# A depthwise convolution on TensorE, regrouped from spans of 8 tokens by 16 channels to spans of 16 tokens by 8 channels, with its matrices spread on chip; z slabs moved; layer norm sums on VectorE

## The chip, the cores and the metric

The kernel runs on all eight cores of one Trainium2 chip, one sequence of the batch on each core, with no exchange between cores. The metric is the time of the slowest core in device microseconds. A program on all eight cores has a second, slower state in some executions (one die at a lower granted TensorE clock). Such runs are marked slow and are left out here. Different chips were used for different groups of runs; each group has its own runs of the kernel before, and ratios are taken inside a group.

Some runs that count as fast are disturbed in a smaller way: one pair of cores shows a mean clock of 0.97 to 0.98 while the others are above 0.98, and the run is some 14 to 22 us longer. This holds for the run of 1688.55 us of e1_runs, that of 1683.27 us of h1_bigpk, and among the runs of the kernel before for the one of 1691.08 us beside e1_runs and four of the seven beside l1_uact. Where a ratio is called "undisturbed" below, these runs are left out; it is the mean of the rest over the mean of the rest, worked out by hand, without an interval.

Engine names in the profile: PE is TensorE (matmul), PEld its weight loads, DVE is VectorE, ACT is ScalarE, POOL is GpSimd, SP is SyncE, which here only issues DMAs. "PEclk" is the granted TensorE clock, 1.00 being full.

## The reference, cut to what matters

```python
xn   = rmsnorm(concat(meta, x), norm_g)               # 16 + 2048 tokens, 2048 channels
v, g, z_c, u, z_s, gl_c, gl_s = split(xn @ w_in)      # 5 x 1024 and 2 x 2048 columns
# branch A: Conformer convolution
a = v * sigmoid(g)
a = causal_depthwise_conv(a, dw_w) + dw_b             # width 31, 1024 channels
a = layernorm(a, ln_g, ln_b)                          # over the 1024 channels
y_c = silu(a) * silu(z_c)
# branch B: S5 state space block (64 groups of 16 channels), gelu, GLU, silu(z_s)
y_s = ...
merged = sigmoid(gl_c + b) * (y_c @ w_conv) + sigmoid(gl_s + b) * (y_s @ w_ssm)
out = rmsnorm(h + merged @ w_out, final_g)[:, 16:]
```

## The kernel before

Everything runs in one pass per core. In time order: x is loaded and normalised while the first projections run (0 to 150 us); then the state space stage (150 to 550 us), in which TensorE alternates between projections (`u`, `vg`, then `z`), the convolution and the state space blocks, and VectorE and ScalarE work for the blocks; then the rest of the `z` slabs, the layer norm and the GLU (to 784 us); then the gates, the two branch projections and the output projection, all 512 columns wide, to the end.

A small list scheduler in the kernel's own source places every instruction on its engine from estimated durations and priorities; the engines then execute these fixed orders.

The convolution is done as banded matrices. The input goes to a scratch tensor in HBM (`a_scr`) and comes back with 8 tokens by 16 channels on the 128 partitions; five 128x128 matrices per group of 16 channels do the 31 taps. The matrices are prepared on the host, mostly zeros, and loaded:

```python
for gp in range(4):                                   # of block m, eight blocks in all
    tz, tzB = TZ[tz_n[0] % 3]
    dma("pool", [(tz, w_dw[4 * m + gp])], ...)        # 320 KB in bf16, twice that in HBM
    z4 = tz.rearrange("p (g d c) -> p g d c", g=2, d=5)
    for gg in range(2):
        g = 2 * gp + gg
        mms([(ps[bk][:, gg * 256:gg * 256 + 256], z4[:, gg, d, :], a3[:, g, 4 - d:260 - d], d == 0, d == 4)
             for d in range(5)], 256, (tzB, a2B), (psB[bk],), prio=14)
    ...                                               # ScalarE moves PSUM out, with scale and bias
```

The layer norm sums over channels, which lie on partitions, are products with a matrix of ones on TensorE, 64 matmuls of 512 columns:

```python
for n in range(4):
    act(sq3, CBv[:, :, n * 512:(n + 1) * 512], AF.Square, n=4096, ...)
    mms([(ps[b1_], ones_b[:, :], CBv[:, m, n * 512:(n + 1) * 512], m == 0, m == 7) for m in range(8)], 512, ...)
    mms([(ps[b2_], ones_b[:, :], sq3[:, m, :], m == 0, m == 7) for m in range(8)], 512, ...)
```

The projections' results leave PSUM through ScalarE or VectorE into small buffers (11 of them, shared), and from there SP issues their stores to scratch:

```python
bk = main_bank()                                      # one of three PSUM banks
proj(wv, wB, 0, lambda k: XMv[:, k, lo:lo + NC], NC, xb_of(lo, lo + NC), bk)
pi, pt, pB = chunk_piece()
cp("act", pt[:, 2:NC + 2], ps[bk][:, 0:NC], n=NC, reads=(psB[bk],), writes=(pB,), prio=1)
dma("sp", [(u_scr[m][j], pt[:, 2:NC + 2])], f"pc{pi}", 128 * NC * 2, (pB,), (uscB[m][j],), prio=5, store=True)
```

## Time and profile before

| | before |
|---|---|
| time, fast runs | 1673.06, 1673.22, 1674.25 us |
| PE busy | 1631 of 1678.5 us |
| state space stage, 150 to 550 us: PE busy, clock | 380 us, 0.97 |
| from 550 us to the gates (784 us) | PE always busy, clock 1.00 |

The first lines are from the page of the kernel before: busy microseconds with the share of the span, then the busy tenths and the granted clock in 40 slices of the span.

```profile
PE 1631.0 (97%) x9426; PEld 928.3 (55%) x9512; DVE 706.7 (42%) x1262; ACT 554.6 (33%) x954; POOL 106.9 (6%) x206
...
PE   7999989998999999999999999999999999999997
...
PEclk9999999999999999999999999999999999999999
```

The table of stretches of the same kernel gives busy time (and number of instructions) of each engine, then clock, DMA share and GB/s.

```profile
core 6: us, PE busy (x) PEld busy (x) DVE busy (x) ACT busy (x) POOL busy (x), PEclk, DMA share, GB/s
...
150.00:550.00 400.00, 379.68 (x3143) 301.20 (x3141) 279.56 (x545) 194.49 (x396) 33.02 (x62) 0.97 0.83 139
550.00:729.20 179.20, 179.03 (x831) 81.34 (x833) 42.73 (x67) 103.98 (x111) 5.81 (x11) 1.00 0.54 133
```

TensorE bounds the kernel; outside the start, what it loses it loses in the state space stage. What it waits for is in the table of waits (total us, times, longest):

```profile
PE ps L446 <- DMA WS<-w_dw: 8.9, 4, 4.2
...
PE ps L446 <- DMA CY<-u_scr: 5.7, 1, 5.7
PE ps L446 <- DVE CY L420: 2.8, 5, 1.0
...
PE ps L446 <- ACT ST L436: 1.0, 1, 1.0
```

And these are groups of instructions, forms kept apart: the convolution's matmuls and the ScalarE copies (busy us, mean ns of one, idle before). The last is the eviction of a `u` tile.

```profile
L446 PE MATMUL ps<-ST,WS 128*128 128x256 bf16 x320 | 41.9, 281 | 10.5 <-DMA WS<-w_dw 8.9 <-DVE ST L437 1.4 <-DVE CY L420 0.2
...
L413 ACT ACTIVATE CY<-SM 128x257 f32<-128x257 f32 x64 | 29.4, 498 | 0.1
...
L413 ACT ACTIVATE CY<-CY,SM 128x514 f32<-128x514 f32 x32 | 22.9, 716 | 0.5
...
L436 ACT CAST ST<-ps 128x258 bf16<-128x258 f32 x64 | 23.7, 372 | 62.5 <-PE ps L446 56.7 <-DMA u_scr<-ST 5.3
```

A mean of a matmul is a latency, not a spacing. The spacing is read from the order in time: ten convolution matmuls of 256 columns start 1.09 us before the next group, 109 ns each.

### The profile page before, as it was taken

To read this page: it belongs to the slowest core of one execution; us is meant where nothing else is said; L and a number is where in the kernel's file an instruction comes from. 1 tells how busy PE (TensorE), PEld (TensorE's weight loads), DVE (VectorE), ACT (ScalarE), POOL (GpSimd) and SP (SyncE) were. 2 spreads that over 40 slices of the span, in tenths; PEclk is the share of its full clock that TensorE was granted. 3 is DMA by queue.
4 is the path that set the end of the run, shared out by engine and by line. 5 is a ranking of instruction groups with operands and counts; after the bars stand their busy time and mean duration, and the time that the engine had idled before them with its cause. 6 is when DMAs were issued, how large, how long until landed. Compare 5 with 4: busy or idle time off the path is not lost.

```text
span 1678.5 us, 25748 instructions; the slowest of 8 cores (1665.3 to 1678.5 us)
## 1 busy us (share of the span) xinstructions
PE 1631.0 (97%) x9426; PEld 928.3 (55%) x9512; DVE 706.7 (42%) x1262; ACT 554.6 (33%) x954; POOL 106.9 (6%) x206
## 2 busy tenths in 40 slices
PE   7999989998999999999999999999999999999997
PEld 6888868887855444444444444444444444444443
DVE  3799158786777110578111111111111221225433
ACT  4564346454455169554111111111111111122222
POOL 1000000010001000000100000000110100100000
PEclk9999999999999999999999999999999999999999
DMA  9935979889577654443644444445555553837612
GB/s 239 218 90 103 144 95 148 143 142 145 110 153 161 160 148 98 113 108 94 113 76 75 76 76 76 76 76 89 100 93 92 101 93 81 184 98 237 215 76 76
DMA packets 115163, 200.86 MB, mean 120 GB/s; under 512 B 19424, under 2 KB 68832, under 8 KB 112864
## 3 DMA queue, kind: packets, MB, share of 16 engines
q0 software_dynamic: 33792, 92.29, 35.2%
q1 hardware_dynamic: 80672, 105.35, 22.9%
q8 instruction: 78, 1.28, 0.3%
q10 hardware_dynamic: 576, 1.58, 0.3%
q14 instruction: 45, 0.37, 0.1%
HBM read 248.92 MB, written 42.53 MB: 174 GB/s over the span
## 4 chain that ended last, share of the span: by engine, by line
PE 89%; DMA 4%; DVE 2%; SPq 2%; issue 2%; ACT 1%; DVEq 0%; ACTq 0%; POOLq 0%
PE ps L446 88%; DMA WS<-w_dw 2%; SPq L458 2%; DVE CY L420 1%; DMA WS<-w_main 1%; DMA CY<-x_t 1%; DMA CY<-u_scr 1%; ACT CY L413 0%; DVE CY L431 0%; PE ps L737 0%; ACT L413 0%; DVE XM L431 0%; DVE ST L431 0%; PE ps L725 0%; DVE CY L979 0%
## 5 line engine op out<-in xcount | busy, mean ns | idle before, releaser
L446 PE MATMUL ps<-XM,WS 128*128 128x258 bf16 (+1 forms) x6144 | 1044.0, 329 | 5.9 <-DVE XM L431 2.2
L446 PEld LDWEIGHTS ps<-XM,WS 128*128 128x128 bf16 x6144 | 603.1, 98 | 409.5 <-issue 12.9
L413 ACT ACTIVATE ST<-ps,SM 128x512 f32<-128x512 f32 (+2 forms) x224 | 137.2, 626 | 622.8 <-PE ps L446 619.2
L431 DVE SCALAR_TENSOR_TENSOR ST<-ps,ST 128x512 f32<-128x512 f32 x132 | 91.3, 692 | 529.1 <-PE ps L446 529.1
L446 PE MATMUL ps<-CY,WS 128*128 128x512 bf16 x1217 | 282.3, 379 | 3.3
L446 PEld LDWEIGHTS ps<-CY,WS 128*128 128x128 bf16 x1280 | 125.1, 98 | 151.1
L420 DVE TENSOR_TENSOR CY<-CY 128x512 bf16<-128x512 f32 (+4 forms) x184 | 120.9, 658 | 28.0 <-PE ps L446 11.4
L413 ACT ACTIVATE ST<-ps 128x258 f32<-128x258 f32 (+1 forms) x136 | 65.0, 483 | 148.7 <-PE ps L446 145.2
L420 DVE TENSOR_TENSOR CY<-ps,CY 128x514 f32<-128x514 f32 (+2 forms) x97 | 66.1, 683 | 109.7 <-PE ps L446 108.8
L413 ACT ACTIVATE CY<-CY 128x514 f32<-128x514 f32 (+3 forms) x112 | 82.3, 751 | 55.9 <-DVE CY L420 30.4
L458 POOL DMA_DIRECT2D WS<-w_main x104 | 55.2, 531 | 684.9 <-PE ps L446 530.2
L420 DVE TENSOR_TENSOR ST<-ST 128x512 f32<-128x512 f32 (+3 forms) x87 | 56.0, 650 | 68.0 <-ACT ST L1090 47.2
L420 DVE TENSOR_TENSOR CY<-CY,ST 128x512 f32<-128x512 f32 (+3 forms) x115 | 64.3, 594 | 14.0 <-DMA CY<-par_b 7.0
L436 ACT CAST ST<-ps 128x258 bf16<-128x258 f32 (+1 forms) x96 | 41.9, 438 | 64.3 <-PE ps L446 58.5
L446 PE MATMUL ps<-CY 128*128 128x256 bf16 (+1 forms) x320 | 52.6, 279 | 8.6 <-DMA CY<-u_scr 5.7
L431 DVE SCALAR_TENSOR_TENSOR XM<-CY,SM,ST 128x258 bf16<-128x258 f32 x128 | 52.8, 483 | 19.2 <-ACT ST L413 19.2
L446 PE MATMUL ps<-XM 128*128 128x512 bf16 (+1 forms) x267 | 56.3, 367 | 0.3
L446 PE MATMUL ps<-CY,XM 128*128 128x512 bf16 x251 | 56.1, 379 | 0.3
L446 PE MATMUL ps<-CY,ST 128*128 128x512 bf16 x251 | 55.2, 380 | 0.3
L446 PE MATMUL ps<-XM,ST 128*128 128x512 bf16 x251 | 55.2, 380 | 0.3
L413 ACT ACT_TABLE_LOAD x35 | 44.9, 1283 | 27.0 <-PE ps L446 13.5
L446 PE MATMUL ps<-ST,WS 128*128 128x256 bf16 x320 | 41.9, 281 | 10.5 <-DMA WS<-w_dw 8.9
(82 smaller groups left out, 799.4 us busy)
## 6 DMA issues: line engine op xcount, KB each, us to landing
WS<-w_main POOLq DMA_DIRECT2D x104, 512.0 KB, 6.3
WS<-w_br POOLq DMA_DIRECT2D x32, 512.0 KB, 6.2
CY<-x_t SPq DMA_DIRECT2D x30, 516.0 KB, 17.6
WS<-w_dw POOLq DMA_DIRECT2D x32, 320.0 KB, 9.5
z_scr<-ST SPq DMA_DIRECT2D x64, 128.0 KB, 3.1
ST<-z_scr SPq DMA_DIRECT2D x32, 256.0 KB, 3.4
WS<-x SPq DMA_DIRECT2D x8, 1024.0 KB, 8.5
CY<-x SPq DMA_DIRECT2D x8, 1024.0 KB, 12.4
```

What stands on the lines that cost most here:

```text
L413: f = lambda e: e.activation(out=out_, in_=in_, func=func, bias=bias, scale=scale)
L420: return S.op(eng, lambda e: e.tensor_tensor(out=out_, in0=in0, in1=in1, op=op), d, reads, writes, **kw)
L431: return S.op("dve", lambda e: e.scalar_tensor_tensor(out=out_, in0=in0, scalar=scalar, in1=in1, op0=op0, op1=op1), 0.15 + n / 960.0, read ...
L436: return S.op("act", lambda e: e.copy(out=out_, in_=in_), 0.22 + n / 1200.0, reads, writes, **kw)
L446: return lambda e: e.matmul(a[0], a[1], a[2], start=a[3], stop=a[4])
L458: return lambda e: e.dma_start(out=o, in_=i, allow_slow_non_contiguous=True)
```

## The change

The intent: with 16 tokens by 8 channels on the partitions, 31 taps need three matrices instead of five, and the moving operand is 128 columns instead of 256. Only the taps are loaded from HBM; ScalarE spreads them into the band matrices by eight copies per half block, each scaled by a column of a 0/1 mask. Four `z` slabs move in among the state space blocks to fill holes of TensorE. The layer norm sums become running sums on VectorE, and TensorE sums only the 128 partitions at the end. The core of the diff:

```diff
-    w_dw = din("w_dw", [32, 128, 1280])
+    w_dw = din("w_dw", [16, 128, 384])
...
-        NPC_, PCB = 11, (NC + 2) * 2
+        NPA, NPU, PCB = 5, 6, (NC + 2) * 2          # store buffers: 5 for a_scr, 6 for u and z
...
-            dma("sp", [(a_scr[m][j], pt)], f"pc{pi}", 128 * PCB, (pB,), (ascB[m][j],), prio=5, store=True)
+            dma("sp", [(a_scr[m][:, j].rearrange("e p c -> p e c"), p3)], f"pa{pi}", 128 * PCB, (pB,), (ascB[m][j],), prio=5,
+                packets=256, store=True)
...
-            for gp in range(4):
-                tz, tzB = TZ[tz_n[0] % 3]
-                dma("pool", [(tz, w_dw[4 * m + gp])], ...)
+            for hf in range(2):
+                tp, tpB = TAP[tz_n[0] % len(TAP)]
+                tz, tzB = TZ[tz_n[0] % 2]
+                dma("pool", [(tp, w_dw[2 * m + hf])], ...)
+                z3 = tz.rearrange("p (x h) -> p x h", h=8)
+                for h in range(8):
+                    act(z3[:, :, h], tp, AF.Copy, scale=mask8[:, h:h + 1], n=384, reads=(tpB, mask8B), parts=(tzB,), prio=15)
+                z4 = tz.rearrange("p (g d c) -> p g d c", g=8, d=3)
+                ...
+                    mms([(ps[bk][:, g * 128:g * 128 + 128], z4[:, 4 * (gq % 2) + g, d, :], a3[:, 4 * gq + g, 2 - d:130 - d], d == 0,
+                          d == 2) for g in range(4) for d in range(3)], 128, (tzB, a2B), (psB[bk],), prio=14)
...
-            if m > 3:
-                vg(m)
+            if 3 <= m < 7:
+                vg(m + 1)
+            for _ in range((1, 1, 1, 1, 0, 0, 0, 0)[m]):
+                z(next(zc))
...
+        for m in range(8):                            # layer norm sums
+            act(s_, c_, AF.Square, bias=dwb(m), n=2048, ...)
+            ...
+                stt(ms, c_, dwb(m), ms, ALU.add, ALU.add, n=2048, ...)
+                tt(vs, vs, s_, ALU.add, n=2048, ...)
```

`z3[:, :, h]`: in bf16 this writes one 2-byte element every 16 bytes. The cut leaves out four smaller parts of the change: the ring of weight slots for the projections shrinks from six to five, the loads of y_scr go to ScalarE's queue, gelu no longer waits for the layer norm, and the scheduler's estimates for short matmuls and transposes are halved.

## The prediction

> **What bounds it now.** TensorE. The page's busy table gives PE 1631 of 1678.5 us (97%); the chain of waits is 88% matmuls. From 550 us on the stretches table shows PE always busy at clock 1.00: 16 matmuls of 512 columns take 3.45 us, 215.8 ns each. The losses lie before: about 29 us at the start (loads, untouched) and the state-space stage, 150 to 550 us, where PE is busy 380 of 400 us at a mean clock of 0.97. Instruction counts times spacings (110 ns for 258 columns, 215.8 for 512) over 150 to 729 us give about 547 of 579 us, so some 32 us are lost to idle and to the low clock behind it. The PE waits name w_dw 8.9 us (longest 4.2), u_scr 5.7 us, VectorE about 4. Other cores lose less (spans from 1665).
>
> **PE work removed.**
> - Convolution: 320 matmuls of 256 columns, 109 ns each = 35 us. After: 384 of 128 columns. Eight 128-column transposes, each with its own weights, span 0.61 us with a latency of 0.22, so 56 ns each: 21.5 us. Saves 13.4.
> - Layer norm sums: 64 matmuls of 512 columns become 16: 48 x 215.8 ns = 10.4 us.
> - Four z slabs as 256-column tiles: under 1 us worse.
> Sum: about 23 us, all on the critical path.
>
> **Stalls.** Conv weights from HBM fall from 32 x 320 KB to 16 x 192 KB, which should remove most w_dw waits and their throttled windows. z slabs fill PE in blocks 0 to 3, where PE stood 5.7 us for u_scr; vg one block earlier takes away waits for a_scr. I expect 15 to 20 of the 32 us back.
>
> **Added, off the path.**
> - ScalarE: 128 spreads of 384 columns. From its 257-column (498 ns) and 514-column (716 ns) copies, about 0.6 us each, 77 us; they write every 16 bytes, and the Trainium skill ("SBUF — State Buffer", the note on 16-byte cachelines) says each new line pays a penalty, so 0.6 to 1.0 us. No instruction of before writes so. ScalarE is busy 194 of 400 us in the stage and would rise to 270 to 320: room, but the convolution now waits for load, then eight spreads, from one tap buffer.
> - VectorE: layer norm sums, 8 x 2.35 + 7 x 2.2 us plus splits, about 43 us, in 550 to 729 us where it is busy 43 of 179; hidden beneath z slabs (166 us for twelve) and the GLU.
> - DMA: a_scr and c_scr rows become 258 and 256 bytes; the skill ("DMA: Bandwidth & Descriptors", Specifications) wants 512. Twice the packets, but less w_dw; only six u/z buffers against 11.9 us landing of a u store could stall PE a few us.
>
> VectorE's work per state-space block is about 38 us, near the block period of 40, so the stage itself ends hardly earlier; the gain appears as more z done inside it, and the gates begin (784 us before) about 40 us earlier. The rest, 890 us, is unchanged.
>
> **Prediction.** 1673 - 23 - 16 = 1634 us, range 1617 to 1652. Faster by over 2%: 0.61; within 2%: 0.36; slower: 0.03.
>
> **Would show it right.** PE busy time down 23 us or more; conv matmuls spaced 56 ns; no w_dw wait on PE; clock 0.98 or better in 150 to 550 us; GLU end near 745 us.
>
> **Would make it wrong.** Conv matmuls spaced near 100 ns (weight loads); PE waiting for spreads on ScalarE, or for u/z buffers behind stores; small-packet DMA delaying u_scr and y loads; layer norm or gelu not finished when z runs out, which would show as PE idle before the GLU or gates.

## The result, and the profile after

Ratios here are the mean time of one kernel's fast runs over that of the other's fast runs of the same rounds, so not quite the ratio of the medians quoted beside them.

| | before | after |
|---|---|---|
| median | 1673.74 us (four runs, one of them slow) | 1784.57 us (1781.28 to 1792.73) |
| ratio, 95% interval | | 1.0669 (1.0632 to 1.0707) |
| PE busy in 150 to 550 us, clock | 380 us, 0.97 | 314 us, 0.89 |
| first matmul of the gates | 784 us | 887 us |

The change made the kernel 6.7% slower. The page of the kernel after:

```profile
PE 1642.4 (92%) x9784; PEld 952.7 (53%) x9784; DVE 749.4 (42%) x1296; ACT 755.0 (42%) x1055; POOL 98.4 (5%) x191
...
PE   7898688877768879999989999999999999999997
...
PEclk9999889989889999999999999999999999999999
```

ScalarE has 200 us more work than before. The slices show where PE has holes now: the third to the fifteenth, which is the state space stage. PE busy went up although it has less to do, because some of it ran at half clock (the granted clock in 220 to 225 us is 0.50; with the spread mended, below, the same 9784 matmuls take 1608.3 us). The stretches:

```profile
150.00:550.00 400.00, 313.63 (x2753) 263.01 (x2751) 220.81 (x440) 312.14 (x397) 15.40 (x29) 0.89 0.46 88
550.00:840.00 290.00, 265.63 (x1597) 153.60 (x1595) 138.57 (x203) 185.35 (x212) 15.87 (x30) 0.98 0.56 120
```

The waits of PE after, where w_dw was first before (L438 is the eviction of `u` tiles, L415 with ST the other evictions, L415 with WS the spread):

```profile
PE ps L448 <- ACT ST L438: 37.4, 15, 6.5
PE ps L448 <- ACT ST L415: 35.2, 14, 7.7
PE ps L448 <- ACT WS L415: 16.2, 4, 8.7
PE ps L448 <- DVE CY L422: 11.8, 6, 9.7
...
PE ps L448 <- DMA WS<-w_br: 7.4, 1, 7.4
```

Two lines of PE's order in time show such waits and the half clock behind them (start, us, what, idle before it). The 24 convolution matmuls take 2.72 us here and 1.51 us at 261.53 us:

```profile
205.95 2.72 PE L448 MATMUL ps<-ST,WS 128*128 128x128 bf16 x24 [8.65 <-ACT WS L415]
...
222.52 3.57 PE L448 MATMUL ps<-XM,WS 128*128 128x256 bf16 x16 [1.13 <-ACT ST L438]
```

And the two groups that explain them, the spread and the eviction of a `u` tile:

```profile
L415 ACT ACTIVATE WS<-CY,SM 128x384 bf16<-128x384 bf16 x128 | 239.9, 2102 | 27.0 <-DMA CY<-w_dw 27.0
...
L438 ACT CAST ST<-ps 128x258 bf16<-128x258 f32 x64 | 30.6, 487 | 16.7 <-PE ps L448 16.5
```

A spread takes 2.10 us, where 0.6 to 1.0 us had been forecast and 0.54 us stands in the kernel's own schedule. PE waits for ScalarE 89 us in these three lines (37.4 + 35.2 + 16.2), and most of that is not for the spreads but for evictions; that these were late because they stood behind spreads is what the experiments test. The eviction itself took 487 ns instead of 372 (369 again in e1_runs); why is not shown.

### The profile page after: what moved, and what is told of

Same layout as the page of the kernel before. It is cut to its first block, busy times and chain, and to the rows that moved or that the text cites. A ratio compares the mean times of both kernels' runs of the same rounds, so it can differ in the third digit from the quotient of the medians.

```text
span 1790.9 us, 26522 instructions; the slowest of 8 cores (1767.2 to 1790.9 us)
## 1 busy us (share of the span) xinstructions
PE 1642.4 (92%) x9784; PEld 952.7 (53%) x9784; DVE 749.4 (42%) x1296; ACT 755.0 (42%) x1055; POOL 98.4 (5%) x191
## 4 chain that ended last, share of the span: by engine, by line
PE 75%; ACT 9%; DMA 6%; issue 4%; DVE 4%; SPq 1%; DVEq 0%; ACTq 0%; POOLq 0%
PE ps L448 75%; ACT WS L415 6%; DVE CY L422 2%; DMA a_scr<-ST 2%; ACT CY L415 1%; DMA CY<-w_dw 1%; DMA ST<-a_scr 1%; DMA WS<-w_main 1%; DVE XM L433 1%; SPq L460 1%; DMA CY<-x_t 1%; ACT ST L438 1%; ACT ST L415 1%; DMA WS<-w_br 0%; DVE CY L1015 0%
## 5 line engine op out<-in xcount | busy, mean ns | idle before, releaser
L448 PE MATMUL ps<-XM,WS 128*128 128x258 bf16 (+2 forms) x6400 | 1062.5, 324 | 59.6 <-ACT ST L415 32.4
L448 PEld LDWEIGHTS ps<-XM,WS 128*128 128x128 bf16 x6400 | 632.9, 99 | 453.6 <-issue 68.4
L415 ACT ACTIVATE ST<-ps,SM 128x512 f32<-128x512 f32 (+1 forms) x160 | 109.6, 687 | 580.6 <-PE ps L448 571.6
L415 ACT ACTIVATE WS<-CY,SM 128x384 bf16<-128x384 bf16 x128 | 239.9, 2102 | 27.0 <-DMA CY<-w_dw 27.0
L448 PEld LDWEIGHTS ps<-CY,WS 128*128 128x128 bf16 x1280 | 125.6, 98 | 160.0 <-issue 10.3
L415 ACT ACTIVATE ST<-ps 128x512 bf16<-128x512 f32 (+2 forms) x184 | 93.1, 513 | 138.7 <-PE ps L448 131.1
L415 ACT ACTIVATE CY<-CY 128x514 f32<-128x514 f32 (+3 forms) x112 | 89.5, 816 | 45.5 <-DVE CY L422 29.6
L422 DVE TENSOR_TENSOR ST<-ST 128x512 bf16<-128x512 f32 (+4 forms) x102 | 77.3, 765 | 69.0 <-ACT ST L415 62.7
L448 PE MATMUL ps<-ST,WS 128*128 128x128 bf16 x384 | 32.8, 259 | 33.1 <-ACT WS L415 16.2
L433 DVE SCALAR_TENSOR_TENSOR ST<-ST,ps 128x258 bf16<-128x258 f32 x64 | 26.8, 420 | 81.8 <-PE ps L448 42.7
L438 ACT CAST ST<-ps 128x258 bf16<-128x258 f32 (+1 forms) x96 | 48.5, 517 | 18.4 <-PE ps L448 18.3
L417 ACT ACTIVATE ST<-WS 128x512 bf16<-128x512 f32 x32 | 20.1, 629 | 84.7 <-DVE WS L422 84.1
```

The costliest lines, as they stand in the source:

```text
L415: f = lambda e: e.activation(out=out_, in_=in_, func=func, bias=bias, scale=scale)
L417: f = lambda e: e.activation(out=out_, in_=in_, func=func, bias=bias, scale=scale, accum_out=accum)
L422: return S.op(eng, lambda e: e.tensor_tensor(out=out_, in0=in0, in1=in1, op=op), d, reads, writes, **kw)
L433: return S.op("dve", lambda e: e.scalar_tensor_tensor(out=out_, in0=in0, scalar=scalar, in1=in1, op0=op0, op1=op1), 0.15 + n / 960.0, read ...
L438: return S.op("act", lambda e: e.copy(out=out_, in_=in_), 0.22 + n / 1200.0, reads, writes, **kw)
L448: return lambda e: e.matmul(a[0], a[1], a[2], start=a[3], stop=a[4])
```

## The experiments

Theory A, at first: the 16-byte stride makes the copy slow; evictions queue behind it; that is all of the 110 us. Rivals: B, small packets and few store buffers; C, the copy is slow for its pointer scale or its bf16 source; and later, an order planned for short spreads (e3_model), ScalarE's load even when mended (F), the store queue.

### The spread with runs of 16 elements (e1_runs)

```diff
-                z3 = tz.rearrange("p (x h) -> p x h", h=8)
+                z3 = tz.rearrange("p (y h t) -> p y h t", h=8, t=16)
                 for h in range(8):
-                    act(z3[:, :, h], tp, AF.Copy, ...)
+                    act(z3[:, :, h, :], tp.rearrange("p (y t) -> p y t", t=16), AF.Copy, ...)
...
-            dma("sp", [(c_scr[m].rearrange("e j (h g) r -> (e j h) (g r)", g=16), c2_)], "c2", ...)
+            dma("sp", [(c_scr[m].rearrange("e j (h g) r -> h (e j) (g r)", g=16), c2_)], "c2", ...)
```

> The changed kernel with only the place of the spread weights changed: each of the eight ScalarE copies of a half writes runs of 16 adjacent elements (32 bytes) instead of one element every 16 bytes, the outputs come out in the order channel, token, and the store to c_scr puts them right. Same number of instructions, same order, right result. Theory A (the stride of the writes made a spread 2.10 us instead of about 0.6, and PSUM evictions queued behind it on ScalarE): the spread falls to 0.6 to 0.8 us, ScalarE busy time falls by 150 us or more, PE waits for ScalarE (88 us now) fall below 20 us, and the time falls by over 100 us to 1625 to 1670. Rival B (small-packet stores, six store buffers for u and z): the spread gets short but the time stays above 1730. Rival C (the copy is slow for the pointer scale or for the bf16 source, not for the stride): the spread stays near 2 us and the time near 1784.

Measured: 1665.64, 1667.24 and 1688.55 us (one more run was slow); before on this chip 1668.70 to 1673.57 us, with one of 1691.08; ratio 0.9987 (0.9878 to 1.0095); result correct. From its groups, page and waits of PE:

```profile
L415 ACT ACTIVATE WS<-CY,SM 128x384 bf16<-128x384 bf16 x128 | 72.1, 608 | 29.0 <-DMA CY<-w_dw 29.0
...
PE 1608.3 (97%) x9784; PEld 937.2 (56%) x9784; DVE 747.1 (45%) x1296; ACT 598.3 (36%) x1055; POOL 98.4 (6%) x191
...
PE ps L448 <- ACT ST L438: 8.2, 3, 3.8
...
PE ps L448 <- ACT ST L415: 3.4, 3, 1.5
```

The spread falls from 2102 to 608 ns with the number and order of the instructions unchanged (only the pattern of the c_scr store changes with it), and over 100 us of the loss go with it. PE's waits for ScalarE in the three lines above fall from 89 to 13 us. Theory A stands; B and C as the main cause fall. PE now has 23 us less work than before (1631.0 to 1608.3), as forecast, and yet the undisturbed runs are only 5 us better than those of the kernel before on this chip (1666.4 against 1671.6 us, 0.997). That second gap is taken up below.

### What one copy costs by its access pattern (e5_bench)

Thirteen dummy instructions, four times over, were put into the gates stage of the kernel before, where ScalarE and VectorE have time. Each form has its own element count, so that it can be told in the profile.

> The kernel before, with copies of about 190 elements added in its gates stage, where ScalarE and VectorE have time, to read what one costs: written to adjacent elements, every 2nd, 4th, 8th, 16th bf16 element, every 16 bytes in float32, in runs of 16, read every 16 bytes, with and without the pointer scale; on VectorE adjacent and every 16 bytes; and the whole spread as one product with a mask on VectorE and on GpSimd. Theory A: adjacent 0.44 us; every 8th element near 1.1 us with either scale, runs of 16 near 0.45. Rival C: every form with a pointer scale slow alike. For strides of 4 and 8 bytes I expect something between.

Measured (busy us, then mean ns of one). On ScalarE: 190 elements written side by side; 189 every 2nd element; 188 every 4th; 187 every 8th, which is the change's pattern; 186 the same with an immediate scale; 185 float32 every 16 bytes; 192 in runs of 16; 90 every 16th; 184 read every 8th and written side by side. On VectorE: 182 side by side, 183 every 8th. Last, half a spread as one product with the mask, on GpSimd and on VectorE.

```profile
L413 ACT ACTIVATE ST<-ST,SM 128x190 bf16<-128x190 bf16 x4 | 1.8, 451 | 9.3 <-POOL ST L420 9.3
L413 ACT ACTIVATE ST<-ST,SM 128x189 bf16<-128x189 bf16 x4 | 2.0, 511 | 0.4
L413 ACT ACTIVATE ST<-ST,SM 128x188 bf16<-128x188 bf16 x4 | 2.9, 714 | 0.4
L413 ACT ACTIVATE ST<-ST,SM 128x187 bf16<-128x187 bf16 x4 | 4.5, 1126 | 0.3
L413 ACT ACTIVATE ST<-ST 128x186 bf16<-128x186 bf16 x4 | 4.1, 1030 | 0.3
L413 ACT ACTIVATE ST<-ST,SM 128x185 f32<-128x185 bf16 x4 | 2.5, 625 | 0.4
L413 ACT ACTIVATE ST<-ST,SM 128x192 bf16<-128x192 bf16 x4 | 1.8, 455 | 0.4
L413 ACT ACTIVATE ST<-ST,SM 128x90 bf16<-128x90 bf16 x4 | 2.7, 679 | 0.4
L413 ACT ACTIVATE ST<-ST,SM 128x184 bf16<-128x184 bf16 x4 | 2.5, 618 | 0.3
...
L425 DVE TENSOR_SCALAR ST<-ST,SM 128x182 bf16<-128x182 bf16 x4 | 1.1, 277 | 0.4
L425 DVE TENSOR_SCALAR ST<-ST,SM 128x183 bf16<-128x183 bf16 x4 | 2.5, 636 | 17.0 <-ACT ST L413 17.0
...
L420 POOL TENSOR_TENSOR ST<-ST,SM 128x1536 bf16<-128x1536 bf16 x4 | 11.2, 2806 | 19.1 <-DVE ST L420 19.1
L420 DVE TENSOR_TENSOR ST<-ST,SM 128x1536 bf16<-128x1536 bf16 x4 | 7.0, 1758 | 0.4
```

The stride of the write is the cause: from every 2nd element on, the cost climbs with the distance, to 2.5 times at 16 bytes (1126 against 451 ns). The pointer scale is worth 96 ns of that (1126 against 1030). Runs of 16 cost nothing. A strided read costs far less than a strided write (618 ns). The distance in bytes is not all: float32 at the same 16 bytes took 625 ns, and at 32 bytes a bf16 element costs no more than at 16 (about 4.2 and 4.4 ns each, if some 0.3 us are fixed, as 451 ns for 190 and 608 for 384 adjacent elements say). The mechanism behind this is not shown.

### The suspected cost alone, added to the kernel before (e4_strided, e4_contig, k5_slots)

```diff
-            s = slot_n[0] % 6                        # weight slots; room for the dummy buffer
+            s = slot_n[0] % 5
...
+                for h in range(5):                   # in each of the 32 convolution steps
+                    act(dz3[:, :, :, h], ones..., AF.Copy, scale=mask8[:, h:h + 1], n=256, ...)   # e4_strided: every 16 bytes
+                    act(dzc[:, h], ones..., AF.Copy, scale=mask8[:, h:h + 1], n=256, ...)         # e4_contig: side by side
```

> The kernel before, with 160 ScalarE copies of 256 bf16 elements added among its convolutions, each writing one element every 16 bytes to a buffer that nobody reads (the weight ring is five slots instead of six to make room). Nothing waits for them but what is behind them on ScalarE. Theory A: about 1.4 us each, ScalarE busy up by about 220 us, and the time up by 40 to 110 us, though no convolution waits for a spread: the evictions behind them are enough. A rival, that it hurts only because the convolution waits for its own spreads: the time stays within 15 us of the kernel before.

> Control of the run with strided copies: the same 160 copies of 256 elements, in the same order, written to adjacent elements. Theory A: 0.5 us each, ScalarE busy up by about 75 us, and the time within 15 us of the kernel before. If five slots or the mere number of ScalarE instructions hurt, this run is slow as well.

> Control for e4_contig (1689 to 1696 us): the kernel before with five weight slots instead of six and no copies. If the 71 us of contiguous copies made e4_contig slow, this is at 1668 to 1677; if the lost slot did it, at about 1690.

The two groups of copies, first of e4_strided (with two of PE's waits there), then of e4_contig:

```profile
L413 ACT ACTIVATE WS<-ones_b,SM 128x256 bf16<-128x256 bf16 x160 | 202.6, 1581 | 15.6 <-DMA WS<-w_dw 15.6
...
PE ps L446 <- ACT ST L436: 32.0, 17, 4.8
...
PE ps L446 <- DMA WS<-w_dw: 2.0, 1, 2.0
```

```profile
L413 ACT ACTIVATE WS<-ones_b,SM 128x256 bf16<-128x256 bf16 x160 | 70.8, 503 | 22.3 <-DMA WS<-w_dw 22.3
```

The strided copies, whose results nobody waits for, make the kernel before slow: 1760.36 us, ratio 1.0497 (1.0417 to 1.0576). The contiguous ones in the same order give 1692.15 us, 1.0093 (1.0014 to 1.0172), 68 us less. (The copies also hold the buffers of w_dw until they have run, but PE waits only 2.0 us for w_dw in e4_strided.) PE waits 44.7 us for evictions there (L436 and L413 with ST) and 13.7 us for other results of ScalarE. So what stands behind the copies on ScalarE, evictions above all, is enough; the wait of the convolution for its own matrices is not needed for the loss. e4_contig is slower than I expected (16 to 21 us instead of under 15), and k5_slots accounts for about half of that: five weight slots alone, without any copies, give 1.0058 (1.0024 to 1.0093), on another chip, and PE is busy 418.4 us of 150 to 600 there against 429.6 before. The change also runs with five slots.

### Was it the order? (e3_model)

The changed kernel with the estimate of a spread raised from 0.54 to 1.89 us, so that the order is planned for slow spreads:

```diff
-                    act(z3[:, :, h], tp, AF.Copy, scale=mask8[:, h:h + 1], n=384, ...)    # n only sets the estimate
+                    act(z3[:, :, h], tp, AF.Copy, scale=mask8[:, h:h + 1], n=2000, ...)
```

> The changed kernel as it is, with its 16-byte stride, but the program that lays out the order of instructions is told that a spread takes 1.9 us instead of 0.54. Rival to theory A (not the 240 us of spreads as such, but an order planned for short ones makes PE wait): the time falls by over 40 us. Theory A: ScalarE keeps 755 us of work, of which over 300 fall into 400 us of the state space stage; the time stays above 1750.

Measured: 1743.40 us, ratio 1.0435 (1.0411 to 1.0460). Both readings are partly right: about 40 us are recovered (1.0669 less 1.0435 is 39 us), which is the mark that I had set for the rival, while the 1750 us that I had set as the least for A were missed; 73 us of loss (1743 less 1670) remain. The state space stage is now well fed (PE busy 443 us of 150 to 600, against 351 in the kernel after), but with less of VectorE's work done (busy 240.5 us of 150 to 600, against 290.4 in e1_runs), and the time comes back later: PE waits for the layer norm.

```profile
PE ps L448 <- DVE ST L422: 41.2, 3, 39.3
PE ps L448 <- ACT ST L415: 27.1, 5, 23.9
```

A better plan moves ScalarE's extra work; it can't remove it.

### Spreading on GpSimd (h4_pool)

On e1_runs, the eight copies are replaced by one product with the mask on GpSimd.

```diff
-                for h in range(8):
-                    act(z3[:, :, h, :], ...)
+                tt(z3, tp.rearrange("p (y t) -> p y t", t=16).unsqueeze(2).broadcast_to(sh),
+                   mask8.unsqueeze(1).unsqueeze(3).broadcast_to(sh), ALU.mult, n=2400, ..., eng="pool")
```

> e1_runs with each half's eight ScalarE copies replaced by one product with the mask on GpSimd, from the bench (2.8 us for 1536 elements) about 5.6 us each, 90 us in all on an engine that is idle for 94% of the time; right result. ScalarE busy falls by 77 us. If ScalarE still holds PE up in e1_runs (13 us of waits), the time falls by 5 to 12 us. If GpSimd and VectorE get in each other's way, VectorE's mean times rise and the time does not fall.

Measured: 1725.36 us, ratio 1.0323 (1.0299 to 1.0346), correct. GpSimd takes 5.5 us a half as expected, and VectorE pays. First two of its groups before, then the same two in h4_pool:

```profile
L420 DVE TENSOR_TENSOR CY<-CY 128x257 f32<-128x257 f32 x64 | 27.4, 428 | 5.7
...
L420 DVE TENSOR_TENSOR CY<-ps,CY 128x514 f32<-128x514 f32 x64 | 43.9, 687 | 61.7 <-PE ps L446 61.7
```

```profile
L422 DVE TENSOR_TENSOR CY<-CY 128x257 f32<-128x257 f32 x64 | 58.1, 907 | 5.7
...
L422 DVE TENSOR_TENSOR CY<-ps,CY 128x514 f32<-128x514 f32 x64 | 43.8, 686 | 65.9 <-PE ps L448 65.9
```

An addition of two SBUF tensors takes 907 instead of 428 ns; one with an operand in PSUM is untouched. This agrees with the Trainium skill, "SBUF — State Buffer", section "Who interferes with whom": VectorE and GpSimd take turns, for whole instructions, on a shared pair of SBUF ports, and a VectorE instruction with two SBUF inputs needs the read port of that pair. The trace shows the turns too: around a GpSimd product of 5.43 us (at 161.79 us) two VectorE operations of 512 columns last 6.53 us, and two of the same form take 1.27 us where GpSimd is idle (at 256.28 us).

### Where the rest of the forecast went: one part of the change at a time

With the write mended the time is at 1667 us, not at 1634. These runs undo or change one thing each; all have the order worked out anew, so a few us between two of them can be the order alone.

```diff
# g3_noz, from e1_runs: no z slabs among the blocks
-            for _ in range((1, 1, 1, 1, 0, 0, 0, 0)[m]):
+            for _ in range((0, 0, 0, 0, 0, 0, 0, 0)[m]):
# g4_lnpe, from e1_runs: layer norm sums on TensorE again, as the 64 matmuls shown above (bias left out of the sums)
# h2_lnonly, from the kernel before: only the layer norm sums on VectorE, gelu not held behind the layer norm
# h1_bigpk, from e1_runs: the store's two runs of 260 bytes as one of 520 (wrong place on purpose)
-            dma("sp", [(a_scr[m][:, j].rearrange("e p c -> p e c"), p3)], f"pa{pi}", ...)
+            dma("sp", [(a_scr[m].rearrange("e j p c -> (e j p c)").rearrange("(j p c) -> j p c", j=8, p=128)[j], pt)], f"pa{pi}", ...)
# g1_buffers, from e1_runs
-        NPA, NPU, PCB = 5, 6, (NC + 2) * 2
+        NPA, NPU, PCB = 5, 8, (NC + 2) * 2
# g5_both, from g1_buffers: gate weights no longer held back
-            return wload(s_, src_ap, 33, after=(zm,) if 6 <= g_slot[0] <= 8 else ())
+            return wload(s_, src_ap, 33)
# k1_two, from h1_bigpk: two of the eight copies, the rest stays zero (wrong on purpose)
-                for h in range(8):
+                for h in range(2):
```

> e1_runs without z slabs among the state space blocks (all sixteen afterwards, as before the change). If the slabs fill holes of PE, the time rises by 5 to 20 us and PE stands idle near 200 us, where it stood for u_scr in the kernel before. If they only take buffers and the store queue from u, the time falls by 3 to 10 us.

> e1_runs with the sums of the layer norm as 64 matmuls on TensorE, as before the change (the convolution bias is left out of the sums, so the result is slightly wrong on purpose). By the count of matmuls PE has 10.4 us more; PE is never idle there, so the time should rise by 10 us, less the 7 us wait for w_br if that goes with VectorE's load: 3 to 11 us above e1_runs.

> One part of the change alone in the kernel before: the layer norm sums on VectorE (and gelu no longer held behind them); convolution, z slabs and their order as before. In g4_lnpe against e1_runs this part was worth about 16 us. If it stands alone, PE busy falls by 10 us and the time falls to 1657 to 1664; then the convolution and the z slabs, with the spread mended, gave nothing (e1_runs has 1667). If the gain of e1_runs over the changed kernel is all of conv, this run is at 1668 or above.

> e1_runs with each store of the gated convolution input as 128 runs of 520 bytes instead of 256 runs of 260 (the place in a_scr is then wrong on purpose, and so is the result; the same bytes are read and computed). Theory E (small packets keep the loads of x longer: in 30 to 150 us PE is busy 114 us of 120 in e1_runs against 118 before, and the DMA share in 100 to 120 us is 0.41 against 0.08): PE busy in 30 to 150 us returns to 117 or more, the a_scr waits (4.6 us) shrink, and the time falls by 4 to 10 us. Rival: the early loss comes from the order of the instructions: no change.

> On top of e1_runs (spreads in runs of 16, 1665.6 and 1667.2 us, one run 1688.6): eight instead of six buffers for the stores of u and z, nothing else by hand; the order of the instructions is worked out anew and differs in places. Theory D (of the 39 us that I forecast, 23 came as PE work, but the stalls did not shrink because u and z wait for six buffers behind stores to HBM): the wait of ScalarE for u_scr stores (11.3 us) and of PE for those evictions (8.2 us, then half clock) nearly vanish, and the time falls by 8 to 15 us to about 1655. Rival: the stores are late because the SP queue is jammed, not because buffers are few: waits move to other tiles and the time stays within 4 us of e1_runs.

> g1_buffers with one more edit: the loads of weights for the first gates no longer wait for the last multiplication of the state space output on VectorE. In e1_runs PE waits 6.9 us for w_br there, because VectorE had 152 us of work in 550 to 785 us (89 in the kernel before) and comes to that multiplication later. Theory: this wait is gone and the time is 6 to 10 us below g1_buffers. Rival: the load was late for the traffic of the DMA, not for that wait: no change.

> h1_bigpk (mended spreads, large packets; 1661 to 1663 us) with two instead of eight copies per half; the rest of the band matrices stays zero from one fill, so the result is wrong on purpose. ScalarE falls by about 58 us, nothing else changes. Theory F (with the stride mended the conv part still gives back its 13 us of PE work because its 77 us on ScalarE delay evictions and tables in a stage where ScalarE is on every chain): 8 to 16 us faster, about 1650. Rival: ScalarE has room at 0.6 us a copy, and the loss lies in the order, the six buffers or the store queue: within 4 us of h1_bigpk.

| run | fast runs, us | ratio (95%) | PE busy, us | PE busy in 30 to 150 / 150 to 600 us |
|---|---|---|---|---|
| before | 1673.06 to 1674.25 | 1 | 1631.0 | 117.9 / 429.6 |
| e1_runs | 1665.64, 1667.24, 1688.55 | 0.9987 (0.9878 to 1.0095) | 1608.3 | 114.5 / 428.5 |
| g3_noz | 1667.19 to 1669.46 | 0.9976 (0.9950 to 1.0002) | 1605.9 | 111.5 / 418.9 |
| g4_lnpe | 1681.11 to 1686.41 | 1.0072 (1.0052 to 1.0092) | 1624.5 | 113.0 / 424.7 |
| h2_lnonly | 1656.88 to 1662.67 | 0.9928 (0.9902 to 0.9953) | 1618.5 | 116.5 / 432.3 |
| h1_bigpk | 1661.31, 1661.69, 1663.44, 1683.27 | 0.9979 (0.9911 to 1.0048) | 1607.8 | 116.6 / 429.1 |
| g1_buffers | 1664.37 to 1672.90 | 0.9978 (0.9951 to 1.0004) | 1613.7 | 111.5 / 426.3 |
| g5_both | 1665.74 to 1673.04 | 0.9981 (0.9954 to 1.0008) | 1612.2 | 112.9 / 428.7 |
| k1_two | 1666.59, 1668.49 (others slow) | none | 1608.8 | 115.9 / 427.6 |

What follows:

- The layer norm sums are the part that pays. Alone in the kernel before they give 0.9928, and taking them out of e1_runs costs about 16 us (3 to 11 had been expected). In h2_lnonly the sums come together with the earlier gelu.
- The z slabs among the blocks gain nothing that can be seen (g3_noz against e1_runs). With them the last VectorE scan of the state space blocks ends at 574 us, without them at 528 us: the slabs are done earlier and the blocks later.
- The convolution, mended, gives back its 13 us. e1_runs is not faster than h2_lnonly, which has the old convolution and 10 us more PE work.
- Part of that may be the small packets. With runs of 520 bytes PE is busy 116.6 us of 30 to 150 instead of 114.5, and the DMA share in 100 to 120 us is 0.09 instead of 0.41: the loads of x are through earlier. In the undisturbed runs this is worth about 3 us (0.995 against 0.997), under the 4 to 10 expected; over all runs the two intervals overlap.
- Another part may be the lost weight slot, which I did not test in the changed kernel. In the kernel before it costs 0.6% (k5_slots), some 10 us, about as much as the convolution gives back; b2_taps, below, which also runs with five slots, has 30 us of idle PE in 150 to 600 us where h2_lnonly has 18.
- ScalarE's load is not the main cause once mended. k1_two leaves away 45 us of ScalarE's busy time, and PE is busy 427.6 us of 150 to 600, no more than in h1_bigpk (429.1). My theory F (8 to 16 us) fell by this stretch. The time leaves room for a smaller share: the mean of its two fast runs is 0.992 of the kernel before on its chip, against 0.995 in the undisturbed runs of h1_bigpk, some 5 us, with no interval and on different chips.
- More buffers move the waits (e1_runs' 8.2 us of PE for `u` evictions become 4.5, but the wait for a_scr grows from 4.6 to 6.7 and one of 4.4 for u_scr appears) and gain nothing. Freeing the gate weights (g5_both) does not move the time either, but it is no test of the wait of 6.9 us for w_br in e1_runs: that wait is gone in g1_buffers already, before the gate weights are freed.

In every one of these versions PE stands idle about 18 to 31 us of 150 to 600 us, as before the change (20 us).

### The store queue (l1_uact, l2_uact), and two versions that did not help (b1_onez, b2_taps)

All scratch stores and loads are issued by SP, in order (after the change, all but the loads of y_scr). In the chain of waits of the kernel before, SP's issues hold 34% of 150 to 220 us. The edit issues the `u` stores from ScalarE's queue, in h2_lnonly and in g5_both:

```diff
-                dma("sp", [(u_scr[m][j], ...)], f"pc{pi}", ...)
+                dma("act", [(u_scr[m][j], ...)], f"pu{pi}", ...)
```

> h2_lnonly with the u stores issued from ScalarE's queue instead of SP's, where they stand behind the issues of other stores and loads. If the jammed SP queue makes the wait for u_scr (6.5 us in h2_lnonly, with half clock behind it), it shrinks below 3 us and the time falls by 4 to 8 us against h2_lnonly's ratio of 0.993, to about 0.989. If ScalarE's issue time costs more than it saves, the ratio is 0.993 or above.

> g5_both (mended spreads, eight u and z buffers, gate weights not held back; ratio 0.998) with the same edit. If the store queue is what keeps PE idle for 20 of 450 us in the state space stage of every version so far (k1_two showed that ScalarE's load is not), PE busy there rises by 6 us or more and the ratio falls to about 0.992. If not, the cause of these 20 us stays open.

Measured: l1_uact 1655.62 to 1658.39 us, correct; before on that chip 1676.24 to 1693.90; ratio 0.983 (0.9774 to 0.9885), by the record's rule unclear. Four of those runs of before are disturbed; undisturbed, the ratio is 0.987, where h2_lnonly on its chip has 0.994 worked out in the same way. l2_uact 1656.76 and 1666.13 us, two more runs slow, so no interval (undisturbed about 0.990). PE busy in 150 to 600 us:

```profile
150.00:600.00 450.00, 437.23 (x3460) 329.31 (x3458) 312.27 (x568) 222.38 (x425) 35.23 (x66) 0.99 0.80 147
```

is l1_uact (432.3 in h2_lnonly), and

```profile
150.00:600.00 450.00, 434.23 (x3852) 351.60 (x3850) 295.55 (x577) 275.65 (x536) 26.97 (x51) 0.98 0.67 125
```

is l2_uact (428.7 in g5_both), just under the 6 us that I had set as the mark. So some 5 us of PE's idle time per version go away when SP no longer issues the `u` stores; it is the only thing tried that shrinks it with either convolution (e3_model's 7 us of idle time there are paid for later). Each figure is of one profile and of an order worked out anew, so I take the 5 us as likely and not as shown: l2_uact loses 2.7 us in 30 to 150 us again (110.2 against 112.9), and PE's wait for u_scr in l1_uact is 4.2 us (6.5 in h2_lnonly), not below 3 as expected. The median time from issue to landing of a `u` store did not fall with it (13.1 us in l1_uact, 10.3 in h2_lnonly); that of the a_scr and u_scr loads, still on SP, did, to 7.6 and 8.7 us from 9.2 and 10.5.

b1_onez adds to h2_lnonly one z slab at the first block, and the gated input one block earlier. b2_taps gives h2_lnonly four buffers for the old convolution matrices, loaded earlier, at the price of one weight slot.

> h2_lnonly (layer norm sums on VectorE alone, 1660 us) with one z slab at the first state space block and the gated input of the convolution one block earlier, as the change has it, and the old convolution. PE waits 6.5 us for u_scr in h2_lnonly; a slab ready to run should fill it: 5 to 8 us faster, 1652 to 1656. If the slab only moves work, 1658 to 1662.

> h2_lnonly with four instead of three buffers for the convolution's weights (five weight slots instead of six) and their loads released after the second store of the block's input instead of the fifth. PE waits 5.6 us for w_dw in h2_lnonly: 3 to 8 us faster if the loads come too late for their buffers; no change or slower if the DMA is the limit or the weight slot is missed.

Measured: b1_onez 1674.33 to 1676.30 us, ratio 0.9959 (0.9920 to 0.9999); b2_taps 1670.95 and 1672.28 us, 0.9936 (0.9884 to 0.9987); before on that chip 1676.80 to 1687.27. In b1_onez PE's wait for u_scr falls to 2.8 us and that for w_dw rises to 12.9; in b2_taps u_scr takes 11.0 us and w_dw is gone. One wait was traded for another, and neither run met the gain that I had set for it.

## Why the prediction was wrong, point by point

- **The step that failed: "so 0.6 to 1.0 us" for a spread, and "room" for it on ScalarE.** It measured 2.10 us, 240 us of busy time instead of 77 to 128. With ScalarE busy 312 of 400 us in the stage, evictions came late, PE waited 89 us for ScalarE and then ran at half clock in parts. e1_runs takes exactly this away and recovers over 100 us; e4_strided puts it, with one weight slot less, into the kernel before and loses over 80, of which 68 are the stride alone (against e4_contig). I had named the risk ("PE waiting for spreads on ScalarE") and seen that no instruction of before writes so; I took a size for it all the same.
- **PE work, 23 us less: right.** PE busy is 1608.3 against 1631.0 us once ScalarE is mended. Its 24 convolution matmuls of 128 columns span 1.51 us with a latency of 0.22, which is 56 ns each, as forecast.
- **"15 to 20 of the 32 us back": wrong.** The waits for w_dw went, and a `u` store landed in 5.4 us (median in e1_runs) instead of 11.9. But PE's idle time in 150 to 600 us is 21.5 us in e1_runs and 20.4 before: evictions behind store buffers and a_scr took its place. That only 5 to 7 of the 39 us came lies in this term, the small packets and the w_br wait, and probably in the lost weight slot, which the forecast does not have at all; how much each takes is not shown.
- **Layer norm on VectorE, hidden: nearly right.** Its sums took 2.29 to 2.35 us each as forecast. With less PE work before the GLU it is no longer fully hidden: w_br waits 6.9 us in e1_runs behind VectorE's last product. It is the part that pays.
- **z slabs filling PE: wrong in effect.** They fill holes and push the blocks back by as much.
- **Small packets: right in direction,** about 3 us in the undisturbed runs, and at the start of the kernel rather than in the stage.
- **The gates "about 40 us earlier":** 24 us in e1_runs (761 against 784 us), as much as the PE work saved.
- **Still open:** what sets the other 13 to 16 us of idle time in the state space stage. Buffers, packets and z slabs do not, ScalarE's mended load not for the most part; the SP queue probably accounts for about 5 us. The changed kernel with six weight slots was not run. That the in-order streams on all engines trade one lateness for another is what the waits suggest; no run shows it.

The best version found is l1_uact: the old convolution, layer norm sums on VectorE, `u` stores from ScalarE's queue; 1.3% faster than the undisturbed runs of the kernel before (1.7% over all its runs, four of which are disturbed).

## What to carry to other kernels

Before moving work to an engine that "has room", measure one instance in its exact access pattern: dtype, write stride, source. An engine that evicts PSUM for TensorE has less room than its busy share says, since whatever stands in front of an eviction delays TensorE, whether or not anyone waits for it. When writes must interleave, choose the order of the output so that each instruction writes runs of adjacent elements (16 bf16 elements here; shorter runs were not measured), and undo the permutation in a DMA that has to run anyway.

## What the Trainium skill lacked or had wrong

- "SBUF — State Buffer", the note on 16-byte cachelines, says that one can stride for free up to 8 bf16 or 4 fp32 elements. ScalarE's writes do not show this: for 187 to 190 bf16 elements 451 ns side by side, 511 ns every 2nd, 714 ns every 4th, 1126 ns every 8th; float32 every 4th took 625 ns for 185. A read of every 8th (618 ns for 184) was not free either. That a penalty exists is right; no size is given, and mine was too small by half or more.
- "ScalarE: Activation LUTs", section "What ACT_TABLE_LOAD costs", gives 280 ns + 0.833 ns per element for an ACTIVATE with one pointer operand. With adjacent writes this holds (438 ns by that figure for 190 elements, 451 measured; 600 for 384, 608 measured), and so does its 93 ns for the pointer (96 measured). It says nothing of the output's stride, which made the same 384 elements take 2102 ns.
- The note on cachelines names no engine and no size. VectorE pays for strided bf16 writes too: 636 ns every 8th element against 277 side by side. Whether all of this is a cost of the stride, or part of it a faster form of the adjacent write, no run here separates.
- "Trainium Kernel Development and Optimization", section "Key Constraints", says that issuing DMAs from several engines only saves the sequencer's issue time. No run here contradicts that, but that section gives no size for what it can be worth: where SP's issues hold 34% of the chain of waits in 150 to 220 us (kernel before), moving the issue of 64 stores took the undisturbed ratio from 0.994 (h2_lnonly, another chip) to 0.987.
